# MLA values on one core: which causal blocks are multiplied whole in f32

## The chip, the cores and the metric

One core of a Trainium2 chip runs the whole program. The metric is the device time of one execution in microseconds; the time before is the median of three runs.

## The reference

A decoder trunk with two layers over 1024 positions of width 1024. Layer 0 mixes tokens with multi-head latent attention (MLA, 12 heads), layer 1 with sliding-window attention; each also has 4 cross-attention heads, an output projection and a squared-ReLU MLP. What this case touches is the causal attention of layer 0:

```python
sc = jnp.einsum('bqhd,bkhd->bhqk', q_blk, k, preferred_element_type=jnp.float32) * scale
mask = k_idx[None, :] <= t_idx[:, None]
sc = jnp.where(mask[None, None], sc, NEG)
p = jax.nn.softmax(sc, axis=-1).astype(v.dtype)
return jnp.einsum('bhqk,bkhd->bqhd', p, v)
```

with 12 heads, keys of 96 and values of 64 elements, all in f32.

## The kernel before

Every large product is made at nearly f32 precision. The usual way is to split each operand in two: a high part (type fp32r, `hi`) and the rest (`lo = x - hi`), and to sum three products, hi x hi, hi x lo and lo x hi. The split is two instructions: a copy on ScalarE (ACT, line 99) and a subtraction on VectorE (DVE, line 100). The other way is one matmul on plain f32 operands, without a split; the profile shows it as two TensorE records. Below it is called "whole".

The attention of layer 0 works with keys in rows and queries in columns. The 1024 queries are two halves G of 512 columns, the keys eight tiles k of 128 rows. A block (G, k) is 128 keys by the queries that may see them: 512 columns wide below the diagonal, and 512, 384, 256 and 128 columns wide for the four diagonal blocks of each half. So (0,2) and (1,6) are 256 wide, (0,3) and (1,7) 128 wide. The 12 blocks of a head follow each other in the order of the list `blocks` (line 851):

(1,0), (0,0), (1,4), (0,1), (1,2), (0,2), (1,5), (0,3), (1,1), (1,6), (1,7), (1,3)

and the last head uses `blocks_end`, in which half 1 comes first. Here "step j" is the j-th block of a head, counted from 0. A step does this:

- `scores` (line 865): three matmuls on the split q and k (line 875; diagonal blocks have a fourth, short one that adds the mask), then on ACT the exponential into the tile `p` (line 885), then for a block that is not whole the split of p into `ph` and `pl`.
- `values` (line 896) for earlier blocks. Three steps after its scores (`LV`) a split block gets its early passes, `vh` x `ph` and `vl` x `ph`; five steps after (`LB`) its late pass, `vh` x `pl`. A whole block gets its one matmul `vf` x `p` three steps after and nothing later. All of them are issued from line 905 into the PSUM tile `pso`.
- `row_max` (line 739): for the next head, the row maxima of the scores, one query tile at a time: one matmul pass and the mask (lines 747, 748), and a reduction on DVE (line 749).
- When the last pass of a half has been issued, ACT copies it out (line 931), and SP sends two DMAs: to the output rows (line 932) and, for the sums in row 64, to `den` (line 937).

Where one of the blocks in work is 128 wide, the score and value passes of a step are issued alternately, else the scores before the values. TensorE (PE) issues in this order; ACT and DVE instructions may have been put in a somewhat different order by the scheduler.

The values of a head come from the tile `v` of the whole stage. `v_tiles` (line 843) splits them for all 8 key tiles into `vh` and `vl`, in two buffers that alternate, at step 6 of the head before. `vh` and `vf` hold ones in columns 64 to 127, so the row sums of the softmax come out of the same matmul. `v_full` (line 994) copies the plain f32 values of all 8 tiles into the single buffer `vf`, at step 8 of the head before. At step 0 of a head `head_tiles` (line 702) loads and splits q and k of the head after next.

`WHOLE` (line 853) names the blocks that are multiplied whole.

Of the kernel before, what the change touches and what calls it, by code (L numbers as in the profile page):

```python
# [9 lines left out]
F32 = mybir.dt.float32  # L10
F32R = mybir.dt.float32r
# [8 lines left out]
P = 128  # L20
D = 1024
S = 1024
NT = S // P
KT = D // P
FF = 4096
H = 12
# [29 lines left out]
def trunk(  # L56
# [7 lines left out]
    nc = tc.nc  # L64
# [4 lines left out]
    def pool(name, side="left", space=None, bufs=1):  # L69
        kw = {"reuse_waits": "tile"}  # L70
        if space is not None:
            kw["space"] = space
        return tc.alloc_tile_pool(name=name, bufs=bufs, side=side, **kw)
# [8 lines left out]
    def ps1(name):  # L82
        return psum[0].tile([P, 512], F32, tag="m", bufs=4 if len(psum) == 1 else 6, name=name)
# [9 lines left out]
    def f32(ap):  # L93
        return ap.bitcast(F32)
# [497 lines left out]
    v = kvp.tile([P, NT, H * 64], F32, name="v")  # L592
# [109 lines left out]
    def head_tiles(h):  # L702
        head_load(h)
        head_split(h)
# [21 lines left out]
    def max_row(h):  # L726
        qh, ql, kh, kl = bufs_[h % 3]
        pt = ps1(f"psxt{h}")[0:8, 0:P]
        nc.tensor.transpose(pt, m8s.pop(h), ident)
        if h:  # L730
            mh, ml = [at.tile([8, P], F32R, tag=f"m{e}", bufs=1, name=f"m{e}{h}") for e in "hl"]
        else:
            mhl = cp.tile([8, 2, P], F32R, tag="krT", bufs=1, name="mhl0")
            mh, ml = mhl[:, 0, :], mhl[:, 1, :]
        split(pt, mh, ml)
        nc.sync.dma_start(out=f32(qh[96:97, :]), in_=f32(mh))
        nc.sync.dma_start(out=f32(ql[96:97, :]), in_=f32(ml))
# [97 lines left out]
    at = pool("at", "right")  # L835
    vbufs = []
    for i in range(2):
        vb = (at.tile([P, NT, 128], F32R, name=f"vh{i}"), at.tile([P, NT, 64], F32R, name=f"vl{i}"))
        vbufs.append(vb)
    vf = at.tile([P, NT, 128], F32, name="vf")  # L840
    nc.gpsimd.memset(vf[:, :, 64:128], 1.0)

    def v_tiles(h):
        vh, vl = vbufs[h % 2]
        src = v[:, :, h * 64 : (h + 1) * 64]
        if h < 2:
            nc.gpsimd.memset(f32(vh[:, :, 64:128]), 1.0)
        nc.scalar.activation(vh[:, :, 0:64], src, AF.Copy)
        nc.vector.tensor_tensor(vl, src, f32(vh[:, :, 0:64]), ALU.subtract)

    blocks = [(1, 0), (0, 0), (1, 4), (0, 1), (1, 2), (0, 2), (1, 5), (0, 3), (1, 1), (1, 6), (1, 7), (1, 3)]

    WHOLE = {(1, 0), (1, 2)}

    blocks_end = [(1, k) for k in (0, 4, 2, 5, 1, 6, 7, 3)] + [(0, k) for k in range(4)]

    def blocks_of(h):
        return blocks if h < H - 1 else blocks_end

    probs, po_ = {}, {}  # L860

    def width(G, k):
        return 512 - max(0, k - 4 * G) * P

    def scores(h, G, k):

        qh, ql, kh, kl = bufs_[h % 3]
        c0 = 512 - width(G, k)
        ks = slice(k * P, (k + 1) * P)
        qs = slice(G * 512 + c0, G * 512 + 512)  # L870
        diag = k >= 4 * G
        ps = ps1(f"pss{h}_{G}_{k}")[:, c0:]

        def mm(o, a, b, **kw):
            return lambda: nc.tensor.matmul(o, a, b, skip_group_check=True, **kw)  # L875

        mms = [mm(ps, kh[:, ks], qh[:, qs], start=True, stop=False)]
        if diag:
            mms.append(mm(ps[:, 0:P], identb, dmaskT, start=False, stop=False))
        mms.append(mm(ps, kh[:, ks], ql[:, qs], start=False, stop=False))  # L880
        mms.append(mm(ps, kl[:, ks], qh[:, qs], start=False, stop=True))

        def then():
            p = at.tile([P, 512], F32, tag="p", bufs=4, name=f"p{h}_{G}_{k}")
            nc.scalar.activation(p[:, c0:], ps, AF.Exp, scale=SC)  # L885
            if (G, k) in WHOLE:
                probs[(h, G, k)] = p
                return
            ph = at.tile([P, 512], F32R, tag="ph", bufs=4, name=f"ph{h}_{G}_{k}")
            pl = at.tile([P, 512], F32R, tag="pl", bufs=5, name=f"pl{h}_{G}_{k}")  # L890
            split(p[:, c0:], ph[:, c0:], pl[:, c0:])
            probs[(h, G, k)] = (ph, pl)

        return mms, then

    def values(h, G, k, late):

        vh, vl = vbufs[h % 2]
        c0 = 512 - width(G, k)
        order = [b[1] for b in blocks_of(h) if b[0] == G]  # L900
        first, last = k == order[0], k == order[-1]
        mms = []

        def mm(o, a, b, **kw):
            mms.append(lambda: nc.tensor.matmul(o, a, b, skip_group_check=True, **kw))  # L905

        if first and not late:
            po_[(h, G)] = ps1(f"pso{h}_{G}")
        po = po_[(h, G)]
        if (G, k) in WHOLE:  # L910
            if late:
                return [], lambda: None
            mm(po[:, c0:], vf[:, k, :], probs.pop((h, G, k))[:, c0:], start=first, stop=last)
        elif late:
            mm(po[:, c0:], vh[:, k, :], probs.pop((h, G, k, "late"))[:, c0:], start=False, stop=last)
        else:
            ph, probs[(h, G, k, "late")] = probs.pop((h, G, k))
            mm(po[:, c0:], vh[:, k, :], ph[:, c0:], start=first, stop=False)
            mm(po[0:64, c0:], vl[:, k, :], ph[:, c0:], start=False, stop=False)
            last = False  # L920

        def then():
            if not last:
                return
            r = slice((h % 2) * 64, (h % 2) * 64 + 64)
            if h == H - 1:
                if G:
                    tails.append(LastHead(G, at.tile([65, 512], F32, tag="on", bufs=2, name="on11"), at.tile([P, 64], F32, tag="den", bufs=2, name="den11")[:, 0:32]))
                return
            on = at.tile([65, 512], F32, tag="on", bufs=2, name=f"on{h}_{G}")  # L930
            nc.scalar.activation(on, po[0:65], AF.Copy)
            nc.sync.dma_start(out=qn[h // 2][r, G * 512 : (G + 1) * 512], in_=on[0:64])
            c = [c for c in range(4) if h >= GRP[c]][-1]
            if c == len(den):
                den_open(c)
            d0 = (h - GRP[c]) * 32 + 16 * G
            nc.sync.dma_start(out=den[c][d0 : d0 + 16, :], in_=on[64:65])

        return mms, then
# [27 lines left out]
    def den_open(c):  # L967
        n = GRP[c + 1] - GRP[c]
        den.append(at.tile([P, 64], F32, tag="den", bufs=2, name=f"den{c}")[: n * 32, 0:32])
        rcd.append(dram.tile([n, S], F32, name=f"rcd{c}"))  # L970
# [21 lines left out]
                nc.vector.tensor_tensor(o, rb, o, ALU.mult)  # L992

    def v_full(h):
        nc.vector.tensor_copy(vf[:, :, 0:64], v[:, :, h * 64 : (h + 1) * 64])

    wq = WoHalf(0, 0, quad_slots())
    v_tiles(0)
# [11 lines left out]
    for n in range(len(seq) + LB):  # L1010
        ms, mv, then = [], [], []
        if n < len(seq):
            ms, then_s = scores(*seq[n])
        for lag, late in ((LB, True), (LV, False)):
            if 0 <= n - lag < len(seq):
                a, b = values(*seq[n - lag], late)
                mv += a
                then.append(b)

        mix = []  # L1020
        if ms and mv and P in [width(*seq[n - lag][1:]) for lag in (0, LV, LB)]:
            while ms and mv:
                mix += [ms.pop(0), mv.pop(0)]
        rows_ = []
        if mix or len(ms) < 4:
            for f in mix + ms:
                f()
            ms = []
        else:

            ms.pop(0)()
        for g, i in ahead.get(n, ()):
            if i < NT:
                rows_.append(row_max(g, i))
            else:
                max_row(g)
        for f in ms:
            f()
        if n < len(seq):
            then_s()  # L1040
        for f in rows_:
            f()
        h, j = divmod(n, NB)
        if n < len(seq):
            if h + 1 < H and j == 6:
                v_tiles(h + 1)
            if h + 1 < H and j == 8:
                v_full(h + 1)
            if j == 0 and h + 2 < H:
                head_tiles(h + 2)  # L1050
        for f in mv:
            f()
        for f in then:
            f()
        next(muls, None)
        if n >= 9 * NB + 8 and n % 3 == 0:
            wq.step()
        for c in range(4):
            if n == GRP[c + 1] * NB + LB + 1:
                rc_out(c)  # L1060
            if n == GRP[c + 1] * NB + LB + 4:
                muls = rc_mul(c)
        if n == len(seq) + LB - 2:
            tails[0].spread(at.tile([P, 512], F32, tag="p", bufs=4, name="rb11"))
# [1016 lines left out]
```

## Time and profile before

| | |
|---|---|
| runs | 2145.73, 2151.09, 2152.23 us; median 2151.09 |
| profiled execution | 2150.26 us, its span 2148.6 us |
| busy: PE | 2100.6 us (98% of the span) |
| busy: PEld, DVE, ACT, POOL | 1709.0, 1475.5, 1149.6, 159.8 us |
| mean granted TensorE clock | 0.997 |
| first and last value matmul start (tile `pso`) | 259.3 and 464.5 us |
| whole value matmuls: records of 128x512 | 48, median 593 ns |
| split value matmuls | 120 each of `vh` x `ph`, `vl` x `ph`, `vh` x `pl` |

PE is TensorE's matmuls, PEld its weight loads, which overlap matmuls. The attention of layer 0 takes about 205 us of the 2148.6, some 17.7 us a head.

### The profile page before, as it was taken

How to read it: one execution, taken by the hardware profiler on the slowest of the kernel's cores; microseconds unless marked ns; L12 is line 12 of the kernel's file. 1: busy time of each engine (PE TensorE's matmuls, PEld its weight loads, DVE VectorE, ACT ScalarE, POOL GpSimd, SP SyncE). 2: the span in 40 equal slices, each digit the busy share in tenths (PEclk: the TensorE clock that was granted, in tenths of full speed). 3: DMA queues.
4: the chain of work that ended last, by engine and by line, in shares of the span. 5: the costliest groups of instructions: out<-in, count | busy, mean ns of one | idle time of the engine just before them, and what ended most of it. 6: DMA issues, size and time to landing. Idle time of an engine off the chain costs nothing.

```text
span 2148.6 us, 29347 instructions
## 1 busy us (share of the span) xinstructions
PE 2100.6 (98%) x10021; PEld 1709.0 (80%) x10021; DVE 1475.5 (69%) x2841; ACT 1149.6 (54%) x2500; POOL 159.8 (7%) x224
## 2 busy tenths in 40 slices
PE   6999999999999999999999999999999999999998
PEld 5888777777788888888888878678888888888887
DVE  7555688864886776786657543766987766886565
ACT  5455477875755444444445553876755453444452
POOL 0012100000000000000001231530000000000000
PEclk9999999999999999999999999999999999999999
DMA  7102223333254445954433211132354446954432
GB/s 252 60 8 60 60 61 80 99 103 134 80 170 153 162 149 177 331 191 137 157 118 94 74 30 50 40 109 84 102 182 142 139 151 202 330 169 146 128 118 89
DMA packets 173729, 275.08 MB, mean 128 GB/s; under 512 B 17189, under 2 KB 72970, under 8 KB 173578
## 3 DMA queue, kind: packets, MB, share of 16 engines
q1 hardware_dynamic: 167008, 256.91, 37.2%
q0 software_dynamic: 4016, 13.12, 1.7%
q10 hardware_dynamic: 2554, 3.17, 0.4%
q8 instruction: 79, 1.29, 0.3%
q14 instruction: 72, 0.59, 0.1%
HBM read 183.79 MB, written 76.86 MB: 121 GB/s over the span
## 4 chain that ended last, share of the span: by engine, by line
PE 83%; DVE 6%; DMA 5%; ACT 4%; issue 1%; POOL 0%; SPq 0%; DVEq 0%; ACTq 0%; POOLq 0%
PE psy L1741 5%; PE psy L1743 5%; PE psy L1742 5%; PE psu L1406 4%; PE psu L1408 4%; PE psu L1407 4%; PE psz L1742 4%; PE psz L1743 4%; PE psz L1741 4%; PE pss L875 4%; PE pso L905 4%; PE psv L1408 3%; PE psv L1407 3%; PE psv L1406 3%; PE pswo L110 2%; PE pswo L108 2%
## 5 line engine op out<-in xcount | busy, mean ns | idle before, releaser
L1306 ACT ACTIVATE mr<-mr,gcol 128x256 f32<-128x256 f32 (+1 forms) x160 | 67.2, 477 | 79.6 <-DMA mr<-in_mlp_w_up_dram 79.5
L1741 PE MATMUL psy<-g 128*128 128x512 f32 x256 | 99.9, 390 | 0.0
L1742 PE MATMUL psy<-g 128*128 128x512 f32 x256 | 99.6, 389 | 0.0
L1743 PE MATMUL psy<-g 128*128 128x512 f32 x256 | 99.3, 389 | 0.0
L1306 ACT ACTIVATE d<-d,gcol 128x256 f32<-128x256 f32 x128 | 57.9, 499 | 76.2 <-DMA d<-in_mlp_w_up_dram 69.7
L99 ACT ACTIVATE g<-i 128x512 fp32r<-128x512 f32 x79 | 49.6, 628 | 88.6 <-PE psz L1742 45.8
L885 ACT ACTIVATE p<-pss 128x384 f32<-128x384 f32 (+3 forms) x144 | 69.8, 486 | 41.2 <-PE pss L875 39.5
L100 DVE TENSOR_TENSOR g<-i,g 128x512 fp32r<-128x512 f32 x79 | 55.4, 701 | 49.1 <-ACT g L99 49.1
L99 ACT ACTIVATE i<-mr 128x512 fp32r<-128x512 f32 x78 | 49.1, 629 | 72.2 <-PE psy L1742 24.7
L99 ACT ACTIVATE uh<-i 128x512 fp32r<-128x512 f32 x66 | 41.6, 630 | 85.5 <-PE psy L1742 40.7
L749 DVE TENSOR_REDUCE m<-psx 128x1 f32<-128x1024 f32 (+7 forms) x96 | 72.0, 752 | 20.6 <-PE psx L748 20.3
L100 DVE TENSOR_TENSOR pl<-p,ph 128x512 fp32r<-128x512 f32 (+3 forms) x120 | 62.2, 526 | 24.4 <-ACT ph L99 22.5
L100 DVE TENSOR_TENSOR uh<-i,uh 128x512 fp32r<-128x512 f32 x66 | 45.5, 689 | 44.2 <-ACT uh L99 44.2
L1743 PE MATMUL psz<-g 128*128 128x512 f32 x192 | 74.7, 389 | 0.0
L1741 PE MATMUL psz<-g 128*128 128x512 f32 x192 | 74.7, 389 | 0.0
L1742 PE MATMUL psz<-g 128*128 128x512 f32 x192 | 74.7, 389 | 0.0
L100 DVE TENSOR_TENSOR i<-mr,i 128x512 fp32r<-128x512 f32 x78 | 53.5, 686 | 22.3 <-ACT i L99 22.1
L99 ACT ACTIVATE ph<-p 128x512 fp32r<-128x512 f32 (+3 forms) x120 | 60.0, 501 | 3.2
L1622 DVE TENSOR_TENSOR mqf<-mqq,mqf 128x512 f32<-128x512 f32 x64 | 43.0, 685 | 22.3 <-DMA mqq<-in_mlp_w_down_dram 22.1
L1743 PEld LDWEIGHTS psy<-g 128*128 128x128 f32 x256 | 48.1, 188 | 10.0
L1741 PEld LDWEIGHTS psy<-g 128*128 128x128 f32 x256 | 48.1, 188 | 9.9
L1742 PEld LDWEIGHTS psy<-g 128*128 128x128 f32 x256 | 48.1, 188 | 9.9
(646 smaller groups left out, 6978.1 us busy)
## 6 DMA issues: line engine op xcount, KB each, us to landing
i<-hd SPq DMA_DIRECT2D x154, 256.0 KB
hd<-uh SPq DMA_DIRECT2D x76, 256.0 KB
hd<-ul SPq DMA_DIRECT2D x76, 256.0 KB
mr<-in_mlp_w_up_dram SPq DMA_DIRECT2D x36, 512.0 KB
hd<-x SPq DMA_DIRECT2D x72, 256.0 KB
mr<-hd SPq DMA_DIRECT2D x70, 256.0 KB
d<-in_mlp_w_up_dram SPq DMA_DIRECT2D x32, 512.0 KB
mqq<-in_mlp_w_down_dram SPq DMA_DIRECT2D x32, 512.0 KB
```

Source lines behind the costliest of these rows:

```text
L99: nc.scalar.activation(hi, src, AF.Copy)
L100: nc.vector.tensor_tensor(lo, src, f32(hi), ALU.subtract)
L749: return lambda: nc.vector.reduce_max(m8s[h][:, i : i + 1], ps[:, :n], axis=AX, negate=True)
L875: return lambda: nc.tensor.matmul(o, a, b, skip_group_check=True, **kw)
L905: mms.append(lambda: nc.tensor.matmul(o, a, b, skip_group_check=True, **kw))
L1306: nc.scalar.activation(w[:, k, :], w[:, k, :], AF.Copy, scale=g_mlp[layer][:, k0 + k : k0 + k + 1])
L1406: nc.tensor.matmul(ps, wh[:, k, :], xh[:, k, :], start=p in (1, 2, 5) and k == 0, stop=False, skip_group_check=True)
L1407: nc.tensor.matmul(ps, wh[:, k, :], xl[:, k, :], start=False, stop=False, skip_group_check=True)
L1408: nc.tensor.matmul(ps, wl[:, k, :], xh[:, k, :], start=False, stop=k == 3, skip_group_check=True)
L1741: nc.tensor.matmul(ps, ah[:, j, :], bh, start=p in (1, 5, 2) and k == 0, stop=False, skip_group_check=True)
L1742: nc.tensor.matmul(ps, ah[:, j, :], bl, start=False, stop=False, skip_group_check=True)
L1743: nc.tensor.matmul(ps, al[:, j, :], bh, start=False, stop=k == NP - 1, skip_group_check=True)
```

## The change

Four other blocks of each head are whole: those of 256 and 128 columns, (0,2), (0,3), (1,6) and (1,7), for (1,0) and (1,2), which are 512 wide and are now split and multiplied in three passes. `vf` therefore holds key tiles 2, 3, 6 and 7, in slots 0 to 3, and is filled with two copies. `vh` and `vl` hold key tiles 0 to 5, which are all that split blocks use. `v_full` is called for the head itself at its step 3 (for head 0 before the loop, as before).

```diff
-        vb = (at.tile([P, NT, 128], F32R, name=f"vh{i}"), at.tile([P, NT, 64], F32R, name=f"vl{i}"))
+        vb = (at.tile([P, 6, 128], F32R, name=f"vh{i}"), at.tile([P, 6, 64], F32R, name=f"vl{i}"))
...
-    vf = at.tile([P, NT, 128], F32, name="vf")
+    vf = at.tile([P, 4, 128], F32, name="vf")
...
-        src = v[:, :, h * 64 : (h + 1) * 64]
+        src = v[:, 0:6, h * 64 : (h + 1) * 64]
...
-    WHOLE = {(1, 0), (1, 2)}
+    WHOLE = {(0, 2): 0, (0, 3): 1, (1, 6): 2, (1, 7): 3}
...
-            mm(po[:, c0:], vf[:, k, :], probs.pop((h, G, k))[:, c0:], start=first, stop=last)
+            mm(po[:, c0:], vf[:, WHOLE[(G, k)], :], probs.pop((h, G, k))[:, c0:], start=first, stop=last)
...
     def v_full(h):
-        nc.vector.tensor_copy(vf[:, :, 0:64], v[:, :, h * 64 : (h + 1) * 64])
+        for i in (0, 2):
+            nc.vector.tensor_copy(vf[:, i : i + 2, 0:64], v[:, i // 2 * 4 + 2 : i // 2 * 4 + 4, h * 64 : (h + 1) * 64])
...
-            if h + 1 < H and j == 8:
-                v_full(h + 1)
+            if h and j == 3:
+                v_full(h)
```

## The prediction

> **What bounds the kernel now.** I read the page first: which engine is busy, and what the chain that ended last is made of.
>
> ```profile
> PE 2100.6 (98%) x10021; PEld 1709.0 (80%) x10021; DVE 1475.5 (69%) x2841; ACT 1149.6 (54%) x2500; POOL 159.8 (7%) x224
> PE 83%; DVE 6%; DMA 5%; ACT 4%; issue 1%; POOL 0%; SPq 0%; DVEq 0%; ACTq 0%; POOLq 0%
> ```
>
> TensorE (PE) is busy for 98% of the span and carries 83% of the chain. That is an average, so the second view is the table by stretch for one head of the attention loop, from the first exponential of head 3 to that of head 4 (columns: length, then busy time and count for PE, PEld, DVE, ACT and POOL, clock, DMA share, GB/s).
>
> ```profile
> 308.56:326.25 17.69, 17.69 (x102) 13.01 (x100) 14.13 (x24) 13.83 (x30) 0.00 (x0) 1.00 0.26 61
> ```
>
> PE is busy for all 17.69 us of the head, at full clock, while DVE has 3.56 us to spare and ACT 3.86 us. The third view, the waits over the eight heads between 290.84 and 433.71, says who is late.
>
> ```profile
> ACT p L885 <- PE pss L875: 26.9, 43, 1.1
> ...
> PEld psx L747 <- DVE m L749: 3.2, 9, 0.7
> ...
> PE psx L747 <- DVE m L749: 0.7, 2, 0.4
> PEld pss L875 <- ACT p L885: 0.4, 1, 0.4
> ```
>
> ACT waits 26.9 us for score matmuls; PE itself waits 0.7 us in eight heads. So a head takes what its matmuls take, and the change is to be priced in PE time. The fourth view is the chain in order of time, which gives what each piece takes from the path (a record's own duration holds a tail that the next matmul overlaps). PE pso is the values, pss the scores.
>
> ```profile
> 311.71 0.06 PE pso L905
> 311.77 0.07 PE pss L875
> 311.84 0.91 PE pso L905 x2
> ...
> 315.66 0.47 PE pso L905 x2
> ...
> 322.14 0.17 PE pso L905
> ...
> 325.37 0.13 PE pso L905
> 325.50 0.24 PE pss L875
> 325.74 0.12 PE pso L905
> 325.86 0.24 PE pss L875
> 326.09 0.24 PE pso L905
> 326.33 0.07 PE pss L875
> 326.40 0.12 PE pso L905
> 326.52 0.28 PE pss L875
> 326.80 0.06 PE pso L905
> 326.87 0.28 PE pss L875
> ```
>
> With the step order of the code these are: 311.71 the late pass of the 128-wide block (1,7); 311.84 the whole 512-wide block (1,0), two records, each of two passes; 315.66 the two early passes of a split 512-wide block; 322.14 the late pass of the 256-wide (0,2); 325.37 and 325.74 the two early passes of the 256-wide (1,6); 326.09 the late pass of a 512-wide block; 326.40 and 326.80 the two early passes of the 128-wide (1,7).
>
> **The change, part by part.** Per head, on PE:
>
> Two whole 512-wide blocks go: 2 x 0.91 = 1.82 us. Two 256-wide split blocks go: 0.13 + 0.12 early and, late, 0.12 (one pass of that width) to 0.17 (the row); I take 0.14, so 0.39 each, 0.78 for both. Two 128-wide split blocks go: 0.12 + 0.06 + 0.06 = 0.24 each, 0.48 for both. Removed: 3.08 us.
>
> Two 512-wide split blocks come: 0.47 early and 0.24 late, 0.71 each, 1.42 for both. Two whole 256-wide blocks come. No such matmul is in this stage, so I bound it: half of the whole 512-wide one is 0.46, and a run of f32 records of exactly this shape (128 rows, 128 columns of weights, 256 wide) stands early in the trace:
>
> ```profile
> 25.73 7.07 PE L329 MATMUL psvm<-wm,memT 128*128 128x256 f32 x32
> ```
>
> That is 0.22 per record, two records a matmul, 0.44. The upper end is 0.52: the whole 512-wide block takes 0.91 where four passes at the 0.22 of one narrower record would be 0.88, and I allow twice that excess per matmul. I take 0.46, 0.92 for both, since this row and the half agree. Two whole 128-wide blocks come: a quarter of 0.91 is 0.23, half of 0.44 is 0.22; the upper end is 0.48, four passes at 0.12, what one 128-wide pass took at 326.40. I take 0.23, 0.46 for both, because at the wider sizes time follows columns. Added: 2.80 us. Net 0.28 us less per head, between 0.40 less (0.44 and 0.22, late 0.17: 2.74 against 3.14) and 0.38 more (0.52 and 0.48, late 0.12: 3.42 against 3.04).
>
> The neighbours: score passes next to a 128-wide value pass take 0.28 where others take 0.24 (326.52 and 326.87 against 325.50); two or three such excesses a head could go with the narrow passes, 0 to 0.10 us. I take 0.05. Together 0.33 us a head, 4.0 us over 12 heads.
>
> ACT and DVE, per head:
>
> ```profile
> L99 ACT ACTIVATE ph<-p 128x512 fp32r<-128x512 f32 x48 | 30.1, 629 | 1.1
> L931 ACT ACTIVATE on<-pso 65x512 f32<-65x512 f32 x22 | 12.8, 584 | 0.0
> ...
> L99 ACT ACTIVATE ph<-p 128x256 fp32r<-128x256 f32 x24 | 10.0, 417 | 0.7
> ...
> L99 ACT ACTIVATE ph<-p 128x128 fp32r<-128x128 f32 x24 | 7.4, 310 | 0.7
> ```
>
> ```profile
> L100 DVE TENSOR_TENSOR pl<-p,ph 128x512 fp32r<-128x512 f32 x48 | 32.8, 686 | 11.9 <-ACT ph L99 11.0
> ...
> L995 DVE COPY vf<-v 128x512 f32<-128x512 f32 x12 | 5.1, 423 | 2.3 <-PE pso L905 2.2
> ```
>
> ACT gets two copies of 629 ns and loses two of 417 and two of 310: 0.20 us less. DVE gets two subtractions of 686 ns, 1.37 us, and loses the four narrow ones, which I leave uncounted; even so it fits into its 3.56 us. v_tiles works on 6 tiles for 8, less on both engines. v_full copies the same values for 4 tiles for 8, in two instructions; with each at most 423 ns that is up to 0.42 us more on DVE. All of this costs nothing while PE waits for neither engine; the cover is the 3.56 and 3.86 us. If it failed in full, it would cost the 1.37 + 0.42 us a head.
>
> Two steps move. v_full goes from step 8 of the head before to step 3 of its own. Its buffer's last reader, (1,7) of the head before, is issued at step 1, its first, (0,2), at step 8, so DVE's queue no longer stands for it (2.2 us in all before, off the path) and PE has five steps. The output of query half 0 now ends with the whole (0,3), read three steps after its scores for five: its ACT copy (584 ns) and its two DMAs on SP are issued two steps earlier, out of the crowded start of the next head into step 10, past the next head's loads on SP's queue; those wait for their own buffers, and nobody reads these two results for some heads. No wait is added on POOL, whose only part is a memset before the loop.
>
> The end of the stage: the last block, (0,3) of head 11, is whole now and needs no subtraction.
>
> ```profile
> 464.49 0.33 PE L905 MATMUL pso<-pl,vh 128*128 128x128 f32 x1 [0.18 <-DVE pl L100]
> ```
>
> This wait of 0.18 us goes; I take 0.2 us. What is late next is the next phase's own operands, which PE then works on as before.
>
> **The sum.** 12 x 0.33 + 0.2 = 4.2 us less. The profiled execution took 2150.26 us (span 2148.6), so 2146.1 by its own time; it lies 0.8 us under the median of 2151.09, against which I predict 2146.9 us.
>
> **A rule beside the rows.** The row: a 512-wide pass takes 0.24 us and the narrowest 0.06 to 0.12. The Trainium skill, page "TensorE: Matmul & The Clock Gate", section "Back-to-back issue gap", gives a sustained spacing of about 81 ns for 128 columns and 131 ns for 512, so a pass costs by its number more than by its width, which speaks against this change. By it (an estimate, with 98 ns for 256 columns by interpolation) a head would lose 2 x (0.081 + 0.098) and gain 2 x 0.131, 0.10 us more per head, 1.2 us more in all. The trace's 0.24 us for 512 columns does not agree with 131 ns.
>
> **The rivals.** *Narrow whole blocks cost by passes, not columns.* For it: 0.12 us for one pass at 326.40, and nothing in this stage shows a narrow f32 matmul. Against it: 0.06 at 311.71 and 326.80, and 0.22 per record at 256. With 0.48 for each of the four, Added is 1.42 + 1.92 = 3.34 against 3.08: 0.26 more per head, 12 x 0.26 - 0.2 = 2.9 us more, 2154.0. The page just named points to this one.
>
> *The narrow blocks free more than their own time.* If the lower ends hold and all score excesses go, 0.40 + 0.10 = 0.50 us a head, 6.0 us, and 0.2 at the end: 2144.9. One thing can add to it. After the stage PE stands for operands and its clock drops:
>
> ```profile
> 492.00:496.00 4.00, 3.85 (x10) 3.08 (x11) 3.11 (x6) 4.00 (x12) 0.00 (x0) 0.60 0.50 147
> ```
>
> A granted clock of 0.60 over 4.00 us loses 1.6 us. If that goes with the shift, 2143.3; it could as well be drawn out by as much, which counts for the range.
>
> *The start of a head becomes crowded (slower).* Block (1,0) is split now, so at step 0 ACT gets 0.63 us and DVE 0.69 us just where both also split the q and k of a later head. If both delays passed on to PE, each head would lose 1.32 us and gain 0.33: 12 x 0.99 - 0.2 = 11.7 us, 2162.8. It decides against the change from a loss of 0.33 us a head on, and is slower by over 0.3% (6.5 us) from 0.33 + 0.55 = 0.88 us on. Against it: the spare 3.56 and 3.86 us, the 584 ns that leave this place on ACT, the 0.7 us of PE waits in eight heads, and that a value pass is issued three to five steps after its scores.
>
> **How the numbers follow.** Two times of this kernel can be told apart from about 0.3%, 6.5 us. The forecast, 2145 to 2149.5, gets 0.56; the narrow blocks freeing more, 2141.5 to 2145, 0.23; cost by passes, 2149.5 to 2154.5, 0.14; crowding, above that, 0.07. Of the second case four fifths, and of the first's own tail some 0.05, lie under 2144.6: faster 0.24, slower 0.07, the same 0.69. The range 2141.5 to 2154.5 leaves out the crowding and some of the tails.
>
> **What would show it.** Right: pieces of 0.43 to 0.52 and 0.21 to 0.28 us in the chain for the whole blocks, 0.47 for the early pair of (1,0), heads about 17.4 us apart, PE still busy through a head, no new PE wait for pl, ph or vf. Wrong: whole 128-wide pieces near 0.48; PE waits for ACT p or DVE m of some tenths a head at its start; a score pass beside a whole narrow block that grows by more than 0.1 us; or a changed stall after the stage that outweighs 4 us.

## The result and the profile after

The changed kernel takes 2144.54 us (median of 7 runs) against 2152.05 for the kernel before on the same chip: the medians are 7.5 us apart. The ratio over all these runs is 0.9973, 95% interval 0.9963 to 0.9984, that is 5.8 us less (3.4 to 8.0). A later comparison gave 0.9985 (0.9976 to 0.9994), 3.2 us less (1.3 to 5.2). The profiled execution has a span of 2142.1 us, 6.5 less than before.

The page of the changed kernel (busy time by engine, and the chain by engine):

```profile
PE 2096.1 (98%) x9997; PEld 1707.2 (80%) x9997; DVE 1471.3 (69%) x2829; ACT 1144.9 (53%) x2476; POOL 160.5 (7%) x224
PE 77%; DMA 7%; DVE 7%; ACT 5%; issue 2%; POOL 0%; SPq 0%; DVEq 0%; ACTq 0%; POOLq 0%
```

PE is as full as before and has 24 records fewer. Its share of the chain is 77% for 83% before, although the time behind the stage turns out to be the same. Where the 6.5 us lie follows from the starts of three matmuls: the first score matmul (`pss`) at 253.8 us before and 253.1 now, the first of the output projection (`pswo`) at 464.7 and 458.1, and the end. So the stretch ahead of the stage gives 0.7 us (other experiments started the stage between 253.1 and 256.5, whatever the change), the stage 210.9 - 205.0 = 5.9 us, and all that follows nothing: 1683.9 and 1684.0 us.

One head of the stage, from the first exponential of head 3 to that of head 4, in the table by stretch (columns as in the prediction):

```profile
307.20:324.59 17.39, 17.39 (x99) 13.17 (x99) 13.80 (x23) 13.42 (x27) 0.00 (x0) 1.00 0.26 62
```

17.69 us have become 17.39, still with PE busy throughout. The waits over the eight heads from head 2 to head 10:

```profile
ACT p L885 <- PE pss L875: 23.2, 37, 1.1
...
PEld pss L875 <- ACT p L885: 1.1, 5, 0.2
PEld pso L905 <- ACT p L885: 0.4, 2, 0.2
PEld psx L747 <- DVE m L749: 0.3, 1, 0.3
```

The reader is to see the last row: weight loads of the row-max matmuls stood 3.2 us for DVE's reductions before, and 0.3 us now. That wait alone is no measure of lost time: in an experiment below (`before_light`), 2.3 us of it remain although every one of these heads there takes about 17.7 us. The waits for ACT, 1.5 us in eight heads for 0.4 before, are of weight loads too, and no wait of PE itself is listed. In the chain in order of time the new pieces are:

```profile
310.19 0.24 PE pso L905
310.43 0.07 PE pss L875
310.50 0.23 PE pso L905
...
320.57 0.27 PE pso L905 x2
...
323.21 0.43 PE pso L905 x2
...
324.66 0.28 PE pso L905 x2
324.93 0.47 PE pss L875 x2
```

310.19 and 310.50 are the early passes of block (1,0), now split, 0.47 us together; 320.57 and 324.66 the whole 128-wide blocks (0,3) and (1,7); 323.21 the whole 256-wide (1,6). The score passes after a whole 128-wide block take 0.47 us for two 512-wide ones, 0.24 each, without the excess of before. On DVE the two copies into `vf` are

```profile
L996 DVE COPY vf<-v 128x128 f32<-128x128 f32 x24 | 5.2, 220 | 0.6 <-PE pso L905 0.6
```

2 x 220 ns for one of 423, so nearly the same.

At the end of the stage the last value passes and the first matmul behind them read, before and now:

```profile
463.98 0.33 PE L905 MATMUL pso<-pl,vh 128*128 128x256 f32 x1
464.49 0.33 PE L905 MATMUL pso<-pl,vh 128*128 128x128 f32 x1 [0.18 <-DVE pl L100]
464.65 0.45 PE L108 MATMUL pswo<-woq,x 128*128 128x512 f32 x1
```

```profile
457.93 0.38 PE L905 MATMUL pso<-p,vf 128*128 128x128 f32 x2
458.07 0.48 PE L108 MATMUL pswo<-woq,x 128*128 128x512 f32 x1
```

Before, the 256-wide late pass and the wait for the last subtraction stood 0.51 us in front of the last pass, where such a pass takes 0.12 to 0.17 in the chain; none of this is left. From the start of the last score matmul to the end of the stage it took 2.20 us before and takes 1.73 now.

### The profile page after: what moved, and what is told of

The parts are those of the page before. It is cut to its first block, busy times and chain, and to the rows that moved or that the text cites. A ratio compares the mean times of both kernels' runs of the same rounds, so it can differ in the third digit from the quotient of the medians.

```text
span 2142.1 us, 29194 instructions
## 1 busy us (share of the span) xinstructions
PE 2096.1 (98%) x9997; PEld 1707.2 (80%) x9997; DVE 1471.3 (69%) x2829; ACT 1144.9 (53%) x2476; POOL 160.5 (7%) x224
## 4 chain that ended last, share of the span: by engine, by line
PE 77%; DMA 7%; DVE 7%; ACT 5%; issue 2%; POOL 0%; SPq 0%; DVEq 0%; ACTq 0%; POOLq 0%
PE psy L1742 5%; PE psy L1744 5%; PE psy L1743 5%; PE pss L875 4%; PE psz L1743 4%; PE psz L1742 4%; PE psz L1744 4%; PE pso L905 4%; DMA d<-in_mlp_w_up_dram 3%; PE psu L1407 3%; DMA mr<-in_mlp_w_up_dram 3%; PE psu L1409 3%; PE psu L1408 3%; PE pswo L110 3%; PE pswo L108 3%; PE pswo L109 3%
## 5 line engine op out<-in xcount | busy, mean ns | idle before, releaser
L100 DVE TENSOR_TENSOR pl<-p,ph 128x512 fp32r<-128x512 f32 x96 | 61.6, 652 | 11.7 <-ACT ph L99 10.0
L99 ACT ACTIVATE ph<-p 128x512 fp32r<-128x512 f32 x96 | 57.4, 601 | 1.8
```

Source lines behind the costliest of these rows:

```text
L99: nc.scalar.activation(hi, src, AF.Copy)
L100: nc.vector.tensor_tensor(lo, src, f32(hi), ALU.subtract)
```

## The experiments

Theory A says that the stage is matmul time, so that the gain is what the two 512-wide blocks cost less when split. Theory B says that the gain is the relief of DVE and ACT, which lose four narrow splits a head. (They get two wide ones for them; in the head shown above DVE is busy 13.80 us for 14.13 before, ACT 13.42 for 13.83.) "Stage" is the length just defined; a "quiet head" is the median distance between the transpositions `psxt`, of which each head has one, over heads 2 to 11. Stage and quiet head are from one profiled execution of each kernel; the changed kernel, run again, gave the same two figures.

| kernel | whole blocks | quiet head | stage | ratio to the kernel before |
|---|---|---|---|---|
| before | (1,0) (1,2) | 17.72 | 210.9 | |
| changed | (0,2) (1,6) (0,3) (1,7) | 17.39 | 205.0 | 0.9973 (0.9963 to 0.9984) |
| `after_again` | the same | 17.39 | 205.0 | 0.9985 (0.9976 to 0.9994) |
| `none_whole` | none | 17.22 | 207.8 | 0.9985 (0.9974 to 0.9996) |
| `six_whole` | all six | 17.59 | 209.3 | 1.0011 (1.0002 to 1.0020) |
| `only_256` | (0,2) (1,6) | 17.37 | 207.4 | 0.9992 (0.9984 to 1.0001) |
| `only_128` | (0,3) (1,7) | 17.15 | 204.0 | 0.9964 (0.9952 to 0.9977) |
| `only_128_again` | (0,3) (1,7) | 17.19 | 203.3 | 0.9963 (0.9949 to 0.9976) |

**No whole block.**

```diff
-    WHOLE = {(0, 2): 0, (0, 3): 1, (1, 6): 2, (1, 7): 3}
+    WHOLE = {}
```

(`vh` and `vl` for 8 tiles again, `vf` gone.)

> Every value block is split, none is multiplied whole. The stage meant is that from the first score matmul of layer 0 to the first matmul of its output projection: 210.9 us before, 205.0 us in the changed kernel. Theory A (the gain is the matmul time of the two 512-wide blocks, 0.91 against 0.71 us; the narrow whole blocks give nothing): the stage keeps the whole gain and is 203.5 to 205.2 us, the time that of the changed kernel or up to 1.5 us less. Theory B (the gain is the relief of DVE and ACT, which lose four narrow splits a head): those come back, 1.4 us a head on DVE and 1.45 us on ACT, PE waits again, the stage is 207 to 211 us and the time 2 to 6 us above the changed kernel's.

The stage, 207.8 us, is in B's interval, and yet the quiet head is 0.17 us shorter than in the changed kernel, as A would have it. The two do not exclude each other: most of the heads of the stage are quiet, and a few are not. During heads 5 and 6 and about heads 9 and 10 DVE has more to do: finished outputs are multiplied by the reciprocal sums (tile `qn`), and the first weights of the output projection are split (tile `woq`). The waits of the kernel without whole blocks between 355 and 373 us:

```profile
PEld pso L903 <- DVE m L749: 1.8, 1, 1.8
DVE qn L990 <- DMA rb<-rcd: 1.4, 1, 1.4
PE pso L903 <- DVE m L749: 1.3, 1, 1.3
```

DVE stands 1.4 us for the DMA that brings the reciprocals to a `qn` multiplication, what follows in DVE's queue, down to a row-max reduction, is late, and PE stands 1.3 us for that. Such heads are called crowded below.

**All six whole**, an edit to the kernel before, with two `vf` buffers of 5 tiles, filled at step 8 of the head before.

```diff
-    WHOLE = {(1, 0), (1, 2)}
+    WHOLE = {(1, 0): 0, (0, 2): 1, (1, 2): 1, (0, 3): 2, (1, 6): 3, (1, 7): 4}
```

> The four narrow blocks and the two 512-wide ones are whole, with two vf buffers. Theory A: the two 512-wide blocks cost what they cost before and the narrow ones about as much as split, so the stage is 210 to 212.5 us and the time within 2 us of the kernel before. Theory B: DVE and ACT are relieved even more than in the changed kernel, the stage is 205 us or less and the time at or under that of the changed kernel.

The stage of 209.3 us lies between the two intervals. The time, 2.4 us over the kernel before (0.4 to 4.3), is just outside A's 2 us and far from B's. It refutes B as the whole cause: DVE and ACT have less to split than in any other of these kernels, and a quiet head takes 0.20 us more than in the changed kernel. Nor does less splitting keep the crowding away. Measured from its first score matmul to that of the next head, head 8 of this kernel takes 18.55 us and head 9 17.99, together 1.4 us over two quiet ones, and the waits between 395 and 436 us show ACT standing for the DMA that brings the projection weights:

```profile
ACT woq L99 <- DMA wor<-in_w_o_dram: 1.8, 2, 1.3
```

**Only the two 256-wide, only the two 128-wide**, with `vh`, `vl`, `vf` and its copies cut to fit.

```diff
+    WHOLE = {(0, 2): 0, (1, 6): 1}
```

```diff
+    WHOLE = {(0, 3): 0, (1, 7): 1}
```

> Only (0,2) and (1,6) are whole. Theory A: the two 512-wide blocks are split, so the stage keeps its gain; a whole 256-wide block takes 0.43 us of the chain against 0.37 to 0.42 split, so the stage is 204.5 to 206 us. Theory B: DVE and ACT get the two 128-wide splits back, 0.56 and 0.62 us a head, the stage is 206 to 208 us.

> Only (0,3) and (1,7) are whole. Theory A: a whole 128-wide block takes 0.28 us against 0.24 split, but its split passes make the score passes beside them wait 0.04 us each, so the stage is 204 to 205.5 us. Theory B: DVE and ACT get the two 256-wide splits back, 0.84 and 0.83 us a head, the stage is 206.5 to 209 us.

Two whole 256-wide blocks cost 0.15 us a quiet head (17.37 against 17.22), two whole 128-wide ones save 0.03 to 0.07. The 256-wide variant still has crowded heads, and its stage falls into B's interval; the 128-wide one is just under both and gives the shortest stage of all. It was run again on another chip:

> Only (0,3) and (1,7) whole, once more on another chip: ratio to the kernel before 0.995 to 0.998, the stage 203.5 to 204.5 us.

Ratio and stage came again, the stage 0.2 us under the stated interval. It beats the kernel before by 0.36 to 0.37%; it was not timed side by side with the changed kernel, but its stage is 1.0 to 1.7 us shorter.

**The extra DVE work on POOL.** The same edit was made in the kernels with no whole block and with only the 128-wide ones:

```diff
-                nc.vector.tensor_tensor(o, rb, o, ALU.mult)
+                nc.gpsimd.tensor_tensor(o, rb, o, ALU.mult)
...
+            if self.layer == 0 and self.half == 0:
+                nc.scalar.activation(hi, raw, AF.Copy)
+                nc.gpsimd.tensor_tensor(lo, raw, f32(hi), ALU.subtract)
...
```

> The kernel with every block split, and the extra work that DVE has in three heads moved to POOL: the multiplication of finished outputs by the reciprocal sums (tile qn, 0.68 us each) and the subtraction of the output-projection weights (tile woq, 1.22 us each). In the kernel with every block split the quiet heads take 17.21 us and those with this extra work 19.3 and 20.1. Theory A and B together (quiet heads by matmul time, crowded heads by DVE): the crowded heads fall to 17.2 to 17.8 us and the stage from 207.8 to 202.5 to 204.5 us. Theory A alone (PE bound everywhere, the long heads owed to the order of the matmuls or to DMAs): they stay at 19 to 20 us and the stage at 207 to 208.

> Only (0,3) and (1,7) whole, and the same extra work on POOL. With only these two whole the stage was 203.95 us and the quiet heads 17.15, with one of 18.1 and 17.7. A and B together: those heads fall to 17.2 to 17.4, the stage to 201.5 to 203.5 us, the time 1 to 2 us under that without the move. A alone: no change of the stage.

Both went the other way: stages of 212.9 and 211.6 us, ratios 0.9997 (0.9987 to 1.0006) and 0.9987 (0.9978 to 0.9997). The timelines of DVE and of POOL, of the first of them, tell why:

```profile
413.32 1.77 DVE L100 TENSOR_TENSOR pl<-p,ph 128x512 fp32r<-128x512 f32 x1
415.02 0.81 DVE L754 TENSOR_REDUCE m<-psx 128x1 f32<-128x640 f32 x1
415.75 2.69 DVE L100 TENSOR_TENSOR pl<-p,ph 128x512 fp32r<-128x512 f32 x1
418.37 0.68 DVE L754 TENSOR_REDUCE m<-psx 128x1 f32<-128x512 f32 x1
418.97 2.24 DVE L100 TENSOR_TENSOR pl<-p,ph 128x512 fp32r<-128x512 f32 x1
```

```profile
412.94 1.60 POOL L995 TENSOR_TENSOR qn<-rb,qn 128x512 f32<-128x512 f32 x1 [51.41 <-DMA rb<-rcd]
415.52 5.14 POOL L646 TENSOR_TENSOR woq<-wor,woq 128x1024 fp32r<-128x1024 f32 x2 [0.97 <-ACT woq L645]
```

A subtraction that takes 0.69 us elsewhere takes 1.77 to 2.69 us while POOL works; each ends about 0.54 us after the POOL instruction that was running when it began, as if it had stood until then. The loss is in this head, 9, which takes 23.2 us from its first score matmul to that of the next, for 17.1 with the work on DVE. Head 6, where DVE no longer stands for the DMA of the reciprocals, fell from 18.9 to 17.4 us, as A and B together would have it. Over the stage, though, the edit did not free DVE, it blocked it, and the stage does not tell A and B apart as meant. It shows B's mechanism from the other side: where DVE is slowed, the stage is 5 to 8 us longer.

**The extra DVE work left out.** In the three light kernels the multiplication by the reciprocal sums is left out, and the low part of the projection weights is a plain copy by DMA.

```diff
-                nc.vector.tensor_tensor(o, rb, o, ALU.mult)
...
+                nc.scalar.activation(hi, raw, AF.Copy)
+                nc.sync.dma_start(out=f32(lo), in_=raw)
...
```

> The kernel before without the extra DVE work of the crowded heads: the multiplication of finished outputs by the reciprocal sums is left out, and the low part of the output-projection weights is a DMA copy of the weights in place of a subtraction. A and B together: the heads of 18.2 and 18.6 us fall to about 17.7, the stage from 210.9 to 209.3 to 210.2 us. A alone: 210.5 to 211.

> The changed kernel with the same work left out. A and B together: its heads were hardly crowded, so the stage falls by less than that of the kernel before, from 205.0 to 204 to 205; what is left between the two light kernels, 12 times the 0.31 us of a quiet head and a few tenths, about 4 to 5 us, is the matmul time of the change, and the rest of the 5.9 us is the relief of DVE. A alone: the two light kernels differ by 5.9 us as the full ones do.

> The kernel with every block split and the same work left out. A and B together: all heads take 17.2 us, the stage falls from 207.8 to 202.5 to 204 us, under that of the changed light kernel. A alone: it stays at 207 to 208 us.

| | full | light |
|---|---|---|
| before: stage | 210.9 | 209.5 |
| changed: stage | 205.0 | 206.0 |
| no whole block: stage | 207.8 | 204.9 |

(One profiled execution each.) By heads, each from its first score matmul to that of the next, the last one to the end of the stage:

| head | before | before, light | changed | changed, light |
|---|---|---|---|---|
| 1 to 4, mean | 17.71 | 17.68 | 17.39 | 17.39 |
| 5 and 6 together | 35.88 | 35.36 | 34.38 | 34.82 |
| 9 and 10 together | 34.53 | 33.74 | 33.15 | 33.81 |
| 11 | 16.52 | 16.52 | 15.51 | 15.51 |

The kernel before loses 1.4 us, nearly all in heads 5, 6, 9 and 10, and its distances between `psxt` from head 2 on all lie between 17.68 and 17.75 us: crowding cost it 1.4 us. The kernel without whole blocks loses 2.8 us, a little less than expected, and falls under the light changed kernel, as expected: crowding is what kept it back. The changed kernel loses nothing; it became 1.0 us longer, against both theories. Of this, 0.66 us lie in heads 9 and 10, where the rows show the reason:

```profile
434.91 1.06 ACT L645 ACTIVATE woq<-wor 128x1024 fp32r<-128x1024 f32 x1 [0.92 <-DMA wor<-in_w_o_dram]
435.87 0.58 ACT L890 ACTIVATE p<-pss 128x512 f32<-128x512 f32 x1
```

```profile
436.50 0.97 PE L880 MATMUL pss<-qk1h,qk1l 97*128 97x512 f32 x3 [0.50 <-ACT p L890]
```

ACT stands 0.92 us for the DMA of the projection weights, the exponential behind it is late, and PE stands 0.50 us for that; the changed kernel itself has no such wait. The other 0.44 us lie in heads 5 and 6, which are 0.2 us shorter each in the changed kernel than its quiet heads; why stays open. Between the light kernels of before and after lie 3.4 us, and 4.1 with the 0.66 us put back.

**The sizes of before.** The changed kernel took 4.2 us less also between the first matmul of the output projection and the first transposition behind it (54.5 us against 58.7), where the kernel before had a stall with the clock at 0.60. In the changed kernel that place reads

```profile
486.00:490.00 4.00, 4.00 (x20) 3.30 (x19) 1.63 (x3) 3.89 (x11) 0.54 (x1) 1.00 0.59 169
490.00:494.00 4.00, 4.00 (x19) 3.32 (x18) 1.83 (x2) 3.59 (x11) 0.54 (x1) 1.00 0.35 105
```

PE full and the clock at 1.00. Smaller tiles, which free memory for the next phase, could be the reason:

```diff
+        vb = (at.tile([P, NT, 128], F32R, name=f"vh{i}")[:, 0:6], at.tile([P, NT, 64], F32R, name=f"vl{i}")[:, 0:6])
+    vf = at.tile([P, NT, 128], F32, name="vf")[:, 0:4]
```

> The changed kernel with vh, vl and vf as large as before, so that all tiles of the stage lie where they lay; the work is the same. It tells what shortened the stretch after the stage, from the first matmul of the output projection to the first transposition of its result (58.7 us before, 54.5 in the changed kernel). Placement (smaller tiles, so that later tiles find free memory earlier): the stretch is 58 to 59 us again, the stage stays at 205. Arrival (the earlier end of the stage, DMAs that no longer collide): the stretch stays at 54 to 55 us.

> The changed kernel again, on the same chip as the three others: ratio to the kernel before 0.996 to 0.9985, the stage 204.5 to 205.5 us, quiet heads 17.4.

With the old sizes the stretch is 55.3 us, with the changed kernel run again 55.1, and the stages are 205.2 and 205.0: it is not the placement (ratios 0.9983, 0.9974 to 0.9992, and 0.9985). What it is stays open. It also buys nothing: over all kernels of this study the time from the end of the stage to the end of the program lies between 1678 and 1686 us, and in the changed kernel it is that of the kernel before.

## Why the prediction was right, and where it was off

The time, 2144.54 us, lies in the range (2141.5 to 2154.5), 2.4 us under the forecast of 2146.9, and by the ratio the verdict is the one held likeliest: faster by 0.27%, under the 0.3% that can be told apart. The later comparison has 0.15%, so the forecast of 4.2 us less lies between the two, inside both intervals. The mechanism named first, PE time in a quiet head, was the right one, but part of the fit is luck: the 0.33 us a head came out because two errors of 0.10 us cancel, as the second point shows. And the median itself falls 0.5 us into the interval of the rival "the narrow blocks free more than their own time" (2141.5 to 2145, chance 0.23), a hair under the 2144.6 set for "faster", and not for that rival's reason: a quiet head gained 0.33 us and not 0.50. What the profiled stage gained beyond the sum came from two other places, the third and the fourth point. Step by step:

- PE is the bound of a quiet head: right. The forecast was 0.33 us a head, measured were 0.30 to 0.33 (17.69 to 17.39 by the exponentials, 17.72 to 17.39 by the median).
- The prices of the pieces: the early pair of a split 512-wide block 0.47 us as predicted; the whole 256-wide 0.43, at the low end of 0.43 to 0.52; the whole 128-wide 0.27 to 0.28, the high end of 0.21 to 0.28. The prices don't add up as the sum assumed: splitting both 512-wide blocks, for which the sum had a gain of 0.40 us, gains 0.50 beside split narrow blocks (17.72 to 17.22) and 0.20 beside whole ones (17.59 to 17.39). Making the four narrow blocks whole costs 0.17 us beside split 512-wide blocks, where the sum had 0.07, and saves 0.13 beside whole ones. Either way round the parts are off and their sum is right. What stands next to a narrow pass, and hides its weight load or not, is part of its price; that is argued from the pieces of 0.24 and 0.28 us, not shown by itself.
- "All of this costs nothing while PE waits for neither engine": this step failed, and a term is missing for it. It was read from eight heads of which most are quiet, and which end where head 10 begins. In the kernel before crowding by the extra work cost 1.4 us of the stage, which the changed kernel does not lose. That it escapes because DVE and ACT split less is not shown: `six_whole` splits least and has the crowding. Of the stage's 5.9 us the light kernels leave 4.1 for the matmuls and the end of the stage, near the predicted 4.2, and about 0.4 open (heads 5 and 6).
- The end of the stage, 0.2 us in the sum: mis-sized. The last head became 1.01 us shorter, 0.7 more than a quiet one, with and without the extra work. With the late pass of the last block go the wait for its subtraction and the standstill around it, 0.47 us behind the last score matmul. The whole 128-wide blocks do most of this: the last head takes 16.17 us without whole blocks and 15.40 with only those two.
- `v_full` was priced at up to 0.42 us more on DVE: it takes 0.44 us in all, for 0.42 before, so hardly anything was added. Its wait shrank from 2.2 to 0.6 us.
- Passes cost by number: refuted, a whole 128-wide block takes 0.28 us and not 0.48. A 512-wide pass takes 0.23 to 0.24 us in the changed kernel too. The 131 ns for 512 columns that the Trainium skill gives, page "TensorE: Matmul & The Clock Gate", section "Back-to-back issue gap", does not agree with that.
- The crowded head start: did not come; the eight heads list no PE wait. The mechanism, DVE behind its queue and PE behind DVE, is real, but in other heads, and in the changed kernel they have lost it.
- The stall after the stage did go, as held possible, and the gain did not last to the end.

The parts of the change that work are the splitting of the 512-wide blocks, which does nearly all in a quiet head, and the whole 128-wide ones, mostly in the last head. The whole 256-wide blocks cost PE 0.15 us a head.

## What to carry to other kernels

Price a change of matmul form by the pieces of the chain in a quiet stretch, and then look separately at the stretches where another engine has extra work: relief there can be worth a quarter of the result, as here 1.4 of 5.9 us, though no average shows it. When a change replaces several things at once, try its parts alone; here one of three parts worked against the other two, and two wrong prices gave a right sum. An idle engine is not a free one: before work is moved to it, look whether it shares something with the one to be relieved.

## What had not been expected of the hardware

POOL's elementwise work on SBUF tiles holds up DVE's. DVE's subtraction of 128x512 took 1.77, 2.69 and 2.24 us beside POOL's multiplication (1.60 us) and subtractions (2.5 us each), for 0.69 without, while DVE's reductions from PSUM kept 0.81 and 0.68 us. All ten 512-wide subtractions in the stage of `none_pool` that began while a POOL instruction ran end 0.54 to 0.55 us after the end of that instruction; the two that had begun before POOL's took 0.68 and 0.69 us. So whoever came second stood. The Trainium skill, page "SBUF — State Buffer", section "Who interferes with whom", says that a DVE instruction with two SBUF inputs contends with a GpSimd instruction that reads SBUF, its second input coming through a read interface that the two share, and that the shared pair of ports is an exclusive lock. These rows agree: the subtraction has two such inputs and the reduction none.
